# A hybrid SSD and attention block on one core: the softmax sums go from VectorE's adds to products of TensorE, the exponentials' products are spread among the projections, and the router's constants come from one product

## The chip, the cores and the metric

The kernel runs on 1 core of one Trainium2 chip. The metric is the device time in microseconds (us) of one execution; the median of 3 runs of the kernel before is 916.55 us (916.28 to 917.62). In the profile PE is TensorE, DVE is VectorE, ACT is ScalarE, POOL is GpSimd and SP is the engine whose queue issues most transfers.

## What is computed

One layer of a diffusion backbone over 512 latent tokens with a prefix of 256 context tokens, in float32: a modulated input projection, a bidirectional state-space scan (SSD), grouped-query attention, one output projection, a layer norm, and a mixture of experts (16 experts, two for each token), with a second layer norm. The change lies in attention and in the constants of the router:

```python
def gqa_block_attention(q, k, v):
    ...
    def one_block(q_blk):
        s = jnp.einsum('bqhgd,bkhd->bhgqk', q_blk, k, preferred_element_type=F32) * scale
        pr = jax.nn.softmax(s, axis=-1).astype(v.dtype)
        return jnp.einsum('bhgqk,bkhd->bqhgd', pr, v)
...
def hier_moe(h, p):
    ...
    g_prob = jax.nn.softmax((t @ p['w_rg'] + p['b_rg']).astype(F32), axis=-1)
    e_logits = (t @ p['w_re'] + p['b_re']).astype(F32).reshape(-1, MOE_GROUPS, EXPERTS_PER_GROUP)
    ...
```

There are 16 query heads on 4 key heads of 64 channels, and 768 keys (256 of the context, 512 latent).

## The kernel before, in words

The block runs in stages: the input projections and the scan (to about 411 us of the profiled span), attention with the output projection (411 to 690 us), the end of the router and the gathering of the tokens (690 to 712 us), then the experts. A list scheduler orders each engine's instructions by a priority (`tc.cur_priority`, which `rank` sets for a block of code) and by which operands and buffers it expects to be ready; each engine then works through its list in that order.

Attention (`attention`, L887) works in 16 units `u`, each one key head `kv` and one tile of 128 queries with the four query heads of that key head. The loop over `i` at L1050 steps through them, four steps to a unit, with several units under way at once. For a unit it does, in turn:

- `scores` (L931), four groups of one query head: a product of 512 and one of 256 keys into PSUM tile `s`, from which DVE takes the maximum of each query (`mx`, L943).
- `shift` (L945): DVE splits the maximum into two parts (`mhl`), TensorE turns them over by a product with the identity into a buffer `b`, and DVE writes the negated rows under the queries (L952).
- `weights` (L958): for each of six blocks of 128 keys two products of 512 columns into a buffer `b`, the first over 128 rows and the second over 72, with the maximum taken off by the last eight rows; ACT writes the exponential to `PT` (L967, tile `hxh`). `pb()` gives the buffers `b`, of which PSUM has two; `shift`, `weights`, the turned queries (`q_turn`, L921) and `finish` share them.
- `values` (L971): for each block two products of 256 columns, each with the 64 channels of `vv` as weights, which write the upper and the lower 64 partitions of tile `v` or `s`. Two blocks are asked for in each of three steps.
- `sums` (L980): DVE adds the six blocks of exponentials in three instructions (`ad`, L982 to L984). `norms` (L986) sums over the keys by 16 products of one column, 32 weight columns each, takes the reciprocal (`rc`) and spreads it (`rcb`).
- `finish` (L998): TensorE turns `rcb` into a buffer `b` (L1001), ACT copies it (`rb`, L1003), DVE multiplies (`o`, L1005), ACT and DVE split the result (`ah`, L1007, `al`, L1008).
- `project` (L1012): for each of two halves `n` of the output columns six products of 512 columns into tile `t`, and DVE adds them to the rows (L1026).

In the table of instructions a product of float32 operands, as `values` and `norms` have them, is two MATMUL entries; a product of float32r operands and a turn is one. All products are recorded at line 107, so groups are told apart by their tiles.

`out_group` for the second half of the scan's rows (`t<-whi,a`) and `router_prep` (L851) are given a place 150 priorities into attention. `router_prep` scales the router's weights by the modulation and the layer norm's gain (L868 to L874, tiles `wrA` and `xo`), and then sums them over the 1024 channels by 2 x 16 products with a tile of ones, 64 weight columns and 20 columns each. The router's constants `ca` and `cb` are read some 160 us later.

Of the kernel before, what the change touches and what calls it, by code (L numbers as in the profile page):

```python
# [8 lines left out]
F32 = mybir.dt.float32  # L9
# [84 lines left out]
def hybrid_block_kernel(ctx: ExitStack, tc: tile.TileContext, I, out):  # L94
# [756 lines left out]
    def router_prep():  # L851
        zero = xo[0][:, 0:256]
# [11 lines left out]
        SP.dma_start(w3[:, :, 4:20], I["w_re"].rearrange("(k p) n -> p k n", p=128))  # L864
        p = pb("t")
# [6 lines left out]
        V.tensor_add(cl[:, 24:32], cl[:, 24:32], cl[:, 8:16])  # L872
        V.tensor_tensor(wrA, w3, cl[:, 16:24, None].to_broadcast([128, 8, 20]), op=OP.mult)
        V.tensor_tensor(tmp, w3, cl[:, 24:32, None].to_broadcast([128, 8, 20]), op=OP.mult)  # L874
        p = pb("t")
        for j, w in enumerate((wrA, tmp)):
            for k in range(8):
                for a in range(2):
                    o = slice(a * 64, a * 64 + 64)
                    mm(p[o, j * 20:j * 20 + 20], ones[:, o], w[:, k], k == 0, k == 7)  # L880
# [4 lines left out]
    LAG, HOLD, WX = 150, 40, 3  # L885

    order = [(kv, t) for kv in (0, 1) for t in range(4)] + [(2, 0), (2, 1), (2, 2), (3, 0), (2, 3), (3, 1), (3, 2), (3, 3)]  # L887

    def attention():
# [6 lines left out]
        k2[0] = eap.tile([128, 2, 768], F32R, name="kT")  # L896
        kT = {}
# [47 lines left out]
        def shift(u):  # L945

            m = wo.tile([128, 8], F32R, name="mhl")
            V.tensor_copy(m[:, 0:4], mx[u])
            V.tensor_sub(m[:, 4:8], mx[u], f32(m[:, 0:4]))
            p = pb("b")[64:72, 0:128]  # L950
            mm(p, f32(m), ident, True, True)
            V.tensor_tensor(qB[u][64:72].rearrange("p (g q) -> p g q", g=4),  # L952
                            p[:, None, :].to_broadcast([8, 4, 128]),
                            minus[:, :, None].to_broadcast([8, 4, 128]), op=OP.mult)
# [3 lines left out]
        def weights(u, ks):  # L958

            kv = order[u][0]  # L960
            if 0 in ks:
                PT[u] = big[:, u % 2]
            for k in ks:
                p, o = pb(), slice(k * 128, (k + 1) * 128)
                mm(p, kT[kv][:, 0, o], qA[u], True, False)
                mm(p, kT[kv][0:72, 1, o], qB[u][0:72], False, True)
                S.activation(PT[u][:, k], p, AF.Exp)  # L967

        po, ad = {}, {}

        def values(u, ks):  # L971
            kv = order[u][0]
            if 0 in ks:
                po[u] = pb("s") if u % 2 else pss.tile([128, 512], F32, name="v")
            for k in ks:
# [36 lines left out]
        def project(u, n):  # L1012
# [19 lines left out]
            if kv == 3:  # L1032
                V.bn_stats(st6[:, t, n, :], us_[t][:, c])

        with rank(rowed):
# [13 lines left out]

        for i in range(4 * 16 + 26):  # L1050
# [3 lines left out]
            if u is not None:  # L1054
# [7 lines left out]
                if g == 3 and u + 1 < 16:  # L1062
                    q_turn(u + 1, qs.pop(u + 1))
            u, g = step(i, 4, 1)
            if u is not None:
                shift(u)
            u, g = step(i, 6, 4)
            if u is not None:
                weights(u, ((0,), (1, 2), (3, 4), (5,))[g])
            u, g = step(i, 10, 4)  # L1070
            if u is not None:
                if g == 0:
                    sums(u)
                if g < 3:
                    values(u, (2 * g, 2 * g + 1))
            u, g = step(i, 14, 1)
            if u is not None:
                rcb[u] = norms(u)
# [3 lines left out]
            u, g = step(i, 18, 2)  # L1082
            if u is not None:
                project(u, g)
# [11 lines left out]
    router_prep()  # L1096
# [578 lines left out]
```

## Time and profile before

| | |
|---|---|
| median of 3 runs | 916.55 us (916.28 to 917.62) |
| profiled execution | 912.09 us, span from first to last instruction 909.8 us |
| PE busy | 819.1 us (90%), 4974 products |
| DVE busy | 696.8 us (77%) |
| ACT busy | 420.2 us (46%) |
| POOL busy | 319.8 us (35%) |
| granted TensorE clock, mean | 0.964 of full speed |

A busy time is the time in which an engine has at least one instruction under way. Products overlap, so what one of them costs is read from its start to the start of the next. Times in the views below count from the first instruction. In a timeline the columns are start, duration, engine, line, operation, out<-in, shape and count, and in brackets the engine's idle time before it with the instruction that ended it. The letters `t`, `b`, `s`, `v` ahead of the arrow are the PSUM tiles named above.

### The profile page before, as it was taken

What the parts mean: (1) busy time and instruction counts of PE and PEld (TensorE: products, weight loads), DVE (VectorE), ACT (ScalarE), POOL (GpSimd) and SP (SyncE); (2) the same over time, 40 slices, a digit from 0 to 9 for tenths busy, and PEclk for the clock granted to TensorE, in tenths of its full rate; (3) what the DMA queues carried; (4) which work ended last, traced back from release to release, by engine and by line L of the source; (5) the groups of instructions that cost most, each with busy time, mean ns of one, the idle gap of its engine ahead of it and who ended that gap; (6) DMA issues with size and microseconds to landing.
All of it is one profiled execution on the core that took longest, in us unless ns stands there. A gap on an engine that the chain in (4) does not pass through costs nothing. (4 is left out here: it accounts for less than half of the span.)

```text
span 909.8 us, 13605 instructions
## 1 busy us (share of the span) xinstructions
PE 819.1 (90%) x4974; PEld 569.0 (63%) x4974; DVE 696.8 (77%) x1074; ACT 420.2 (46%) x776; POOL 319.8 (35%) x230
## 2 busy tenths in 40 slices
PE   6999998899989999999988999899982799999992
PEld 2696676556776566776655656556652577777762
DVE  3575764886967897656776787877888999899977
ACT  2253443545563144453541444444433466776652
POOL 0012211426231273410059036540314555545524
PEclk9999999999999999999997999999996799999997
DMA  9966996436343133676053011120185999999974
GB/s 300 319 195 235 286 303 215 128 116 185 104 118 83 45 118 109 202 227 170 24 151 103 13 30 62 46 83 1 53 273 207 332 350 340 331 339 343 338 212 192
DMA packets 112349, 165.54 MB, mean 182 GB/s; under 512 B 13144, under 2 KB 78200, under 8 KB 112280
## 3 DMA queue, kind: packets, MB, share of 16 engines
q1 hardware_dynamic: 105560, 141.24, 48.8%
q0 software_dynamic: 6288, 21.84, 8.4%
q10 hardware_dynamic: 432, 1.57, 0.5%
q8 instruction: 39, 0.64, 0.3%
q14 instruction: 30, 0.25, 0.1%
HBM read 142.41 MB, written 22.21 MB: 181 GB/s over the span
## 5 line engine op out<-in xcount | busy, mean ns | idle before, releaser
L75 ACT ACTIVATE whi<-wraw 128x1024 fp32r<-128x1024 f32 (+1 forms) x100 | 104.1, 1045 | 74.7 <-PE a L107 40.8
L76 DVE TENSOR_TENSOR wlo<-wraw,whi 128x1024 fp32r<-128x1024 f32 (+1 forms) x73 | 94.7, 1303 | 24.0 <-ACT whi L75 23.3
L967 ACT ACTIVATE hxh<-b 128x512 f32<-128x512 f32 x96 | 55.7, 595 | 88.9 <-PE b L107 88.2
L76 POOL TENSOR_TENSOR wlo<-wraw,whi 128x1024 fp32r<-128x1024 f32 (+1 forms) x22 | 53.5, 2432 | 117.9 <-ACT whi L75 98.5
L943 DVE TENSOR_REDUCE mx<-s 128x1 f32<-128x768 f32 x64 | 61.0, 953 | 34.3 <-PE s L107 34.2
L473 DVE SCALAR_TENSOR_TENSOR acc<-u,cols,acc 128x770 f32<-128x770 f32 (+1 forms) x48 | 56.8, 1182 | 28.5 <-ACT acc L465 23.0
L107 PE MATMUL a<-whi,hxh 128*128 128x512 f32 (+2 forms) x176 | 70.7, 403 | 1.8 <-ACT hxh L263 1.8
L107 PE MATMUL a<-wlo,hxh 128*128 128x512 f32 (+2 forms) x176 | 69.8, 397 | 0.2 <-DVE wlo L76 0.2
L107 PE MATMUL a<-whi,hxl 128*128 128x512 f32 (+2 forms) x176 | 69.1, 394 | 0.0
L107 PE MATMUL a<-hxl,whi 128*128 128x512 f32 (+1 forms) x176 | 64.5, 367 | 0.0
L107 PE MATMUL a<-hxh,whi 128*128 128x512 f32 (+1 forms) x176 | 64.1, 364 | 0.0
L107 PE MATMUL a<-hxh,wlo 128*128 128x512 f32 (+1 forms) x176 | 63.9, 363 | 0.0
L590 ACT ACTIVATE bc<-bc,lb 128x128 f32<-128x128 f32 x128 | 40.6, 392 | 13.5 <-POOL bc L587 13.3
L107 PE MATMUL a<-whi,xh 128*128 128x512 f32 x102 | 43.8, 429 | 0.0
L1435 POOL DMA_INDIRECT acc<-y,rowi x15 | 26.5, 1768 | 48.5 <-DVE wlo L76 29.6
L107 PE MATMUL a<-wlo,xh 128*128 128x512 f32 x102 | 41.1, 402 | 0.1
L107 PE MATMUL a<-whi,xl 128*128 128x512 f32 x102 | 40.9, 401 | 0.0
L107 PEld LDWEIGHTS a<-whi,hxh 128*128 128x128 f32 x176 | 33.9, 193 | 10.9 <-issue 4.2
L107 PEld LDWEIGHTS a<-wlo,hxh 128*128 128x128 f32 x176 | 34.0, 193 | 9.7 <-issue 4.9
L107 PEld LDWEIGHTS a<-hxh,wlo 128*128 128x128 f32 x176 | 33.9, 193 | 9.2 <-issue 5.3
L107 PEld LDWEIGHTS a<-whi,hxl 128*128 128x128 f32 x176 | 33.7, 192 | 9.3 <-issue 4.6
L107 PEld LDWEIGHTS a<-hxl,whi 128*128 128x128 f32 x176 | 34.0, 193 | 7.4 <-issue 3.6
(489 smaller groups left out, 2169.4 us busy)
## 6 DMA issues: line engine op xcount, KB each, us to landing
wraw<-in_w_mod_dram SPq DMA_DIRECT2D x32, 512.0 KB
wraw<-in_w_in_dram SPq DMA_DIRECT2D x30, 512.0 KB
wraw<-in_w_down_dram SPq DMA_DIRECT2D x22, 512.0 KB
wraw<-in_w_gate_dram SPq DMA_DIRECT2D x40, 256.0 KB
wraw<-in_w_up_dram SPq DMA_DIRECT2D x40, 256.0 KB
mraw<-in_w_mod_dram SPq DMA_DIRECT2D x32, 256.0 KB
bc<-csd SPq DMA_DIRECT2D x32, 256.0 KB
wraw<-in_w_out_dram SPq DMA_DIRECT2D x8, 512.0 KB
```

Of the source, the lines that this page charges most:

```text
L75: self.nc.scalar.activation(hi, raw, AF.Copy)
L76: self.lo_engine(i).tensor_sub(lo, raw, hi.bitcast(F32))
L107: return PE.matmul(o, lhsT=a, rhs=b, start=first, stop=last)
L473: V.scalar_tensor_tensor(a, uk, wk_, a, op0=OP.mult, op1=OP.add)
L590: S.activation(bc[:, d, h, :], bc[:, d, h, :], AF.Exp, bias=lb[:, c, h0 + h:h0 + h + 1])
L943: V.tensor_reduce(mx[u][:, g:g + 1], pss_[:, 768 * i:768 * i + 768], axis=AX, op=OP.max)
L967: S.activation(PT[u][:, k], p, AF.Exp)
L1435: G.indirect_dma_start(out=acc, out_offset=bass.IndirectOffsetOnAxis(ap=rows, axis=0), in_=y, in_offset=None, compute_op=OP.add)
```

## The change

It has three parts. (1) `sums` and the tile `ad` are gone. `values` now does all 12 products of a unit in one run, and behind them 48 products of one column (64 weight columns of `PT` against a column of ones), which sum the exponentials of all six blocks in PSUM; `norms` keeps only the reciprocal and `rcb`. The run has the rank of attention's start and is held until the last product of `weights` that was written before it. (2) `weights` does one block for each call, and a step sets one or two blocks between the four halves of `project`, which is now a generator; `shift` writes the split maximum into a part of the constants' tile and turns 72 columns over with one transpose; `finish` stands ahead of `weights`. (3) `router_prep` is a generator whose parts come at steps 18, 21, 24 and 27; DVE sums the scaled weights over the eight blocks of channels, and one product with ones, 40 columns wide, does the rest.

```diff
     def router_prep():
...
+        yield
         p = pb("t")
         PE.transpose(p[:, 0:32], rw[0:32, 0:128], ident[0:32, 0:32])
...
+        yield
         V.tensor_tensor(wrA, w3, cl[:, 16:24, None].to_broadcast([128, 8, 20]), op=OP.mult)
         V.tensor_tensor(tmp, w3, cl[:, 24:32, None].to_broadcast([128, 8, 20]), op=OP.mult)
+        wsum = wr[:, 352:392]
+        for j, w in enumerate((wrA, tmp)):
+            V.tensor_reduce(wsum[:, j * 20:j * 20 + 20], w.rearrange("p k n -> p n k"), axis=AX, op=OP.add)
+        yield
         p = pb("t")
-        for j, w in enumerate((wrA, tmp)):
-            for k in range(8):
-                for a in range(2):
-                    o = slice(a * 64, a * 64 + 64)
-                    mm(p[o, j * 20:j * 20 + 20], ones[:, o], w[:, k], k == 0, k == 7)
+        mm(p[:, 0:40], ones, wsum, True, True)
+        yield
...
+    PREP = (18, 21, 24, 27)
...
         def shift(u):
-            m = wo.tile([128, 8], F32R, name="mhl")
-            V.tensor_copy(m[:, 0:4], mx[u])
-            V.tensor_sub(m[:, 4:8], mx[u], f32(m[:, 0:4]))
-            p = pb("b")[64:72, 0:128]
-            mm(p, f32(m), ident, True, True)
+            V.tensor_copy(mhl[:, 64:68].bitcast(F32R), mx[u])
+            V.tensor_sub(mhl[:, 68:72].bitcast(F32R), mx[u], mhl[:, 64:68])
+            p = pb("b")[:, 0:128]
+            PE.transpose(p[0:72], mhl, ident)
+            p = p[64:72]
...
-        def values(u, ks):
+        def values(u):
             kv = order[u][0]
-            if 0 in ks:
-                po[u] = pb("s") if u % 2 else pss.tile([128, 512], F32, name="v")
-            for k in ks:
-                for gp in range(2):
-                    mm(po[u][gp * 64:gp * 64 + 64, 0:256], vv[:, k, kv * 64:(kv + 1) * 64],
-                       PT[u][:, k, gp * 256:gp * 256 + 256], k == 0, k == 5)
-        def sums(u):
-            a = ad[u] = wo.tile([128, 3, 512], F32, name="ad", bufs=1)
-            V.tensor_add(a, PT[u][:, 0:3], PT[u][:, 3:6])
-            V.tensor_add(a[:, 0], a[:, 0], a[:, 1])
-            V.tensor_add(a[:, 0], a[:, 0], a[:, 2])
+            p = po[u] = pb("s") if u % 2 else pss.tile([128, 512], F32, name="v")
+            with rank(first), tc.issue_after(held["weights"].ins):
+                for k in reversed(range(6)):
+                    for gp in range(2):
+                        mm(p[gp * 64:gp * 64 + 64, 0:256], vv[:, k, kv * 64:(kv + 1) * 64],
+                           PT[u][:, k, gp * 256:gp * 256 + 256], k == 5, k == 0)
+                for g in range(4):
+                    for k in range(6):
+                        for o in (0, 64):
+                            mm(p[o:o + 64, 256 + g:257 + g], PT[u][:, k, g * 128 + o:g * 128 + o + 64], ones[:, 0:1], k == 0, k == 5)
         def norms(u):
-            a = ad.pop(u)
-            for g in range(4):
-                for o in range(0, 128, 32):
-                    mm(po[u][o:o + 32, 256 + g:257 + g], a[:, 0, g * 128 + o:g * 128 + o + 32], ones[:, 0:1], True, True)
...
             for kk in range(2):
                 mm3(p, h[:, kk], l[:, kk], wh[:, kk], wl[:, kk], kk == 0, kk == 1)
+                if kk == 0:
+                    yield
...
+            u, g = step(i, 16, 1)
+            if u is not None:
+                finish(u, rcb.pop(u))
+                proj[u] = outs(u)
             u, g = step(i, 6, 4)
-            if u is not None:
-                weights(u, ((0,), (1, 2), (3, 4), (5,))[g])
...
+            ks = () if u is None else ((0, 1), (2,), (3, 4), (5,))[g]
+            v, h = step(i, 18, 3)
+            for j in range(2):
+                if j < len(ks):
+                    weights(u, ks[j])
+                if v is not None and (h, j) != (2, 1):
...
+                    next(proj[v], None)
+            u, g = step(i, 11, 1)
             if u is not None:
-                project(u, g)
+                values(u)
+            u, g = step(i, 13 if i < 72 else 12, 1)
+            if u is not None and u not in rcb:
+                rcb[u] = norms(u)
```

How the instructions stand shows at three places. A row is one instruction, or several in a row with their count, with its line, its operation, out<-in and shape, and the semaphores that it waits for (named after the engine or the DMA queue that raises them).

TensorE in the middle of attention, before, from the turn of one unit's maximum to the first products of `norms`; `s<-hxh,hxl` are `values`, `b<-hxl` are `weights`, `s<-kT,hxl` are `scores`, L1001 is the turn in `finish`:

```order
L107 MATMUL b<-cst,mhl 8x128 [waits DVE_49,Activation_49]
L107 MATMUL b<-hxl 128x512 [waits Activation_49]
L107 MATMUL b<-hxl 128x512
L107 MATMUL s<-hxh,hxl 64x256 x3
L107 MATMUL b<-hxl 128x512 [waits Activation_49]
L107 MATMUL b<-hxl 128x512
L107 MATMUL s<-hxh,hxl 64x256
L107 MATMUL s<-kT,hxl 128x256 [waits DVE_49]
L107 MATMUL s<-kT,hxl 128x512
L1001 MATMUL b<-cst,rcb 128x128 [waits DVE_49]
L1001 MATMUL b<-cst,rcb 128x128
L107 MATMUL s<-ones,ad 32x1 x5
```

The same engine now, at the run of one unit's values; `v<-ones,hxh` are the new sums, `t<-whi,ah` and the rows like it are `project`:

```order
L107 MATMUL b<-hxl 128x512 [waits Activation_49]
L107 MATMUL b<-hxl 128x512
L107 MATMUL v<-hxh,hxl 64x256 x12
L107 MATMUL v<-ones,hxh 64x1 x48
L107 MATMUL t<-whi,ah 128x512 [waits DVE_49]
```

The 12 products of values stand together, where they were parted into runs of 4, 3, 1 and 4, and the 48 one-column products follow them without another kind of product between.

TensorE now, from one unit's `shift` (L957) and the turn in `finish` (L1000) over the next products of `weights`:

```order
L957 MATMUL b<-cst 72x128 [waits DVE_49,PE_49,Activation_49]
L1000 MATMUL b<-cst,rcb 128x128 [waits Activation_49]
L1000 MATMUL b<-cst,rcb 128x128
L107 MATMUL b<-hxl 128x512 [waits Activation_49]
L107 MATMUL b<-hxl 128x512
L107 MATMUL s<-kT,hxl 128x256 [waits DVE_49]
L107 MATMUL s<-kT,hxl 128x512
L107 MATMUL b<-hxl 128x512 [waits Activation_49]
L107 MATMUL b<-hxl 128x512
L107 MATMUL b<-hxl 128x512 [waits DVE_49]
L107 MATMUL b<-hxl 128x512
```

The two turns now stand back to back, where before products of `weights` and `values` stood between them; of the next three pairs of `weights` two wait for ACT and the third for DVE.

DVE at the router's constants, before; L868 to L874 are `router_prep`, `mx<-s` are the maxima of `scores`, `mhl` and `qs` belong to `shift` and `q_stack`:

```order
L868 COPY xo<-t 128x32 [waits PE_49]
L943 TENSOR_REDUCE mx<-s 128x1
L869 TENSOR_SCALAR xo<-xo 128x8 [waits DVE_49]
L948 CAST mhl<-mx 128x4 [waits DVE_49]
L871 TENSOR_TENSOR xo<-xo 128x8 [waits DVE_49]
L871 TENSOR_TENSOR xo<-xo 128x8
L949 TENSOR_TENSOR mhl<-mx,mhl 128x4 [waits DVE_49]
L873 TENSOR_TENSOR wrA<-xo 128x160 [waits DMAHW3_49,DMAHW2_49,DVE_49]
L872 TENSOR_TENSOR xo<-xo 128x8 [waits DVE_49]
L874 TENSOR_TENSOR xo<-xo 128x160 [waits DVE_49]
L917 TENSOR_TENSOR qs<-q,qs 128x4x64 [waits DMAHW2_49,PE_49,Activation_49]
```

And now; L870 to L880 are `router_prep`, L1027 is the add of `project`:

```order
L870 COPY xo<-t 128x32 [waits PE_49]
L871 TENSOR_SCALAR xo<-xo 128x8 [waits DVE_49]
L950 TENSOR_REDUCE mx<-s 128x1 [waits PE_49]
L873 TENSOR_TENSOR xo<-xo 128x8 [waits DVE_49]
L873 TENSOR_TENSOR xo<-xo 128x8
L876 TENSOR_TENSOR wrA<-xo 128x160 [waits DMAHW3_49,DVE_49]
L874 TENSOR_TENSOR xo<-xo 128x8 [waits DVE_49]
L1027 TENSOR_TENSOR x<-x,t 128x512 [waits PE_49]
L877 TENSOR_TENSOR xo<-xo 128x160 [waits DVE_49]
L880 TENSOR_REDUCE xo<-wrA 128x20
L880 TENSOR_REDUCE xo<-xo 128x20 [waits DVE_49]
L950 TENSOR_REDUCE mx<-s 128x1 [waits PE_49]
```

The add of one half of `project` (L1027) now stands behind six of the router's instructions, and the next maximum behind three more.

## Rows read from the trace of the kernel before

**Rows 1.** Busy time by stretch: bounds, length; PE, PEld, DVE, ACT, POOL; clock, DMA.

```profile
410.00:490.00 80.00, 71.89 (x429) 46.99 (x429) 57.08 (x74) 29.60 (x50) 27.43 (x15) 0.94 0.40 114
490.00:650.00 160.00, 153.94 (x1145) 95.81 (x1144) 122.90 (x185) 68.53 (x139) 53.82 (x28) 0.99 0.13 39
650.00:690.00 40.00, 34.37 (x302) 22.63 (x301) 33.79 (x79) 16.62 (x29) 12.18 (x12) 0.91 0.69 237
```

**Rows 2.** Timeline of PE over one unit of attention.

```profile
554.34 0.50 PE L107 MATMUL t<-whi,ah 128*128 128x512 f32 x1
...
557.17 1.08 PE L107 MATMUL s<-hxh,hxl 128*64 128x256 f32 x8
558.18 0.50 PE L107 MATMUL t<-whi,ah 128*128 128x512 f32 x1
...
560.59 0.39 PE L107 MATMUL b<-cst,mhl 128*8 128x128 f32 x2
560.90 0.73 PE L107 MATMUL b<-hxl,kT 128*128 128x512 f32 x2
561.56 1.08 PE L107 MATMUL s<-hxh,hxl 128*64 128x256 f32 x6
562.57 0.73 PE L107 MATMUL b<-hxl,kT 128*128 128x512 f32 x2
563.23 0.65 PE L107 MATMUL s<-hxh,hxl 128*64 128x256 f32 x2
563.81 0.62 PE L107 MATMUL s<-kT,hxl 128*128 128x256 f32 x2
...
564.58 0.29 PE L107 MATMUL s<-ones,ad 128*32 128x1 f32 x10
564.79 1.20 PE L107 MATMUL b<-hxl,kT 128*128 128x512 f32 x4
...
566.27 1.08 PE L107 MATMUL v<-hxh,hxl 128*64 128x256 f32 x8
567.29 0.36 PE L107 MATMUL s<-ones,ad 128*32 128x1 f32 x22
567.58 0.50 PE L107 MATMUL t<-whi,ah 128*128 128x512 f32 x1
```

**Rows 3.** Timeline of PE at one tile's router logits (64 weight columns, 20 columns each).

```profile
680.44 1.11 PE L107 MATMUL t<-wrA,xo 128*64 128x20 f32 x32
681.48 0.50 PE L107 MATMUL s<-whi,ah 128*128 128x512 f32 x1
```

**Rows 4.** Timeline, a product of weights to its exponential, a turn to its copy.

```profile
574.11 0.74 PE L107 MATMUL b<-hxl,kT 128*128 128x512 f32 x2
...
574.89 0.60 ACT L967 ACTIVATE hxh<-b 128x512 f32<-128x512 f32 x1 [1.92 <-PE b L107]
...
577.48 0.38 PE L1001 MATMUL b<-cst,rcb 128*128 128x128 f32 x2
...
577.90 0.38 ACT L1003 ACTIVATE rb<-b 128x256 f32<-128x256 f32 x1 [0.75 <-PE b L1001]
```

**Rows 5.** Waits of PE from 410 to 690 us: total, times, longest.

```profile
PE t L107 <- DVE wrA L873: 3.5, 1, 3.5
PE b L107 <- DVE mhl L949: 3.3, 3, 1.4
PE t L107 <- DVE xo L874: 3.3, 1, 3.3
PE s L107 <- DVE o L1005: 1.9, 1, 1.9
PE t L107 <- DVE y L1026: 1.4, 1, 1.4
```

**Rows 6.** Timeline of DVE, two adds of the same shape.

```profile
525.80 0.69 DVE L983 TENSOR_TENSOR ad<-ad 128x512 f32<-128x512 f32 x1
...
527.01 2.67 DVE L984 TENSOR_TENSOR ad<-ad 128x512 f32<-128x512 f32 x1
```

More of the change, by code (lines that the diff above doesn't have):

```diff
@@ L896, in attention @@
         k2[0] = eap.tile([128, 2, 768], F32R, name="kT")
+        mhl = rows[:, 0:72]
+        V.memset(mhl[:, 0:64], 0.0)
         kT = {}
@@ L956, in attention, with weights @@
         PT = {}
-        def weights(u, ks):
+        def weights(u, k):
             kv = order[u][0]
-            if 0 in ks:
-                PT[u] = big[:, u % 2]
-            for k in ks:
[L964 to L969, printed above, removed]
-        def values(u, ks):
-            kv = order[u][0]
-            if 0 in ks:
-                po[u] = pb("s") if u % 2 else pss.tile([128, 512], F32, name="v")
-            for k in ks:
-                for gp in range(2):
-                    mm(po[u][gp * 64:gp * 64 + 64, 0:256], vv[:, k, kv * 64:(kv + 1) * 64],
-                       PT[u][:, k, gp * 256:gp * 256 + 256], k == 0, k == 5)
@@ L980, in sums @@
-        def sums(u):
-            a = ad[u] = wo.tile([128, 3, 512], F32, name="ad", bufs=1)
-            V.tensor_add(a, PT[u][:, 0:3], PT[u][:, 3:6])
-            V.tensor_add(a[:, 0], a[:, 0], a[:, 1])
-            V.tensor_add(a[:, 0], a[:, 0], a[:, 2])
+            PT[u] = big[:, u % 2]
+            p, o = pb(), slice(k * 128, (k + 1) * 128)
+            mm(p, kT[kv][:, 0, o], qA[u], True, False)
+            held["weights"] = mm(p, kT[kv][0:72, 1, o], qB[u][0:72], False, True)
+            S.activation(PT[u][:, k], p, AF.Exp)
@@ new lines, in attention @@
+        po = {}
+        def values(u):
+            kv = order[u][0]
+            p = po[u] = pb("s") if u % 2 else pss.tile([128, 512], F32, name="v")
[8 more added lines that the diff above has]
+                            mm(p[o:o + 64, 256 + g:257 + g], PT[u][:, k, g * 128 + o:g * 128 + o + 64], ones[:, 0:1], k == 0, k == 5)
@@ L1033, in project @@
                 V.bn_stats(st6[:, t, n, :], us_[t][:, c])
+            yield
+        first = tc.cur_priority
         with rank(rowed):
@@ L1048, in step, with outs @@
             return (u, g) if 0 <= u < 16 and g < n else (None, None)
+        proj = {}
+        def outs(u):
+            for n in range(2):
+                yield from project(u, n)
         for i in range(4 * 16 + 26):
@@ L1063, in attention @@
                     q_turn(u + 1, qs.pop(u + 1))
+            if i in PREP:
+                next(prep, None)
             u, g = step(i, 4, 1)
@@ L1066, in attention @@
                 shift(u)
-            u, g = step(i, 6, 4)
-            if u is not None:
-                weights(u, ((0,), (1, 2), (3, 4), (5,))[g])
[L1070 to L1078, printed above, removed]
             u, g = step(i, 16, 1)
@@ L1081, in attention @@
                 finish(u, rcb.pop(u))
-            u, g = step(i, 18, 2)
+                proj[u] = outs(u)
+            u, g = step(i, 6, 4)
+            ks = () if u is None else ((0, 1), (2,), (3, 4), (5,))[g]
[4 more added lines that the diff above has]
+                if v is not None and (h, j) != (2, 1):
+                    if (h, j) == (1, 0):
+                        pass
+                    next(proj[v], None)
+            u, g = step(i, 11, 1)
             if u is not None:
-                project(u, g)
+                values(u)
+            u, g = step(i, 13 if i < 72 else 12, 1)
+            if u is not None and u not in rcb:
+                rcb[u] = norms(u)
             u, g = step(i, 19, 4)
@@ L1095, in hybrid_block_kernel @@
             out_group(1, n)
-    router_prep()
+    prep = router_prep()
+    next(prep)
     tc.cur_priority = at
```

## The prediction

> **What bounds the kernel now.** I read the busy time by stretch first. From 490 to 650 us, the middle of attention, PE is busy 153.94 of 160 us and DVE 122.90 [rows 1], so PE's own work sets the pace, and DVE matters where PE waits for it. Next comes PE's timeline over one unit: from 554.34 to 567.58 us, 13.24 us, PE has no idle time in any row shown [rows 2]. Last come PE's waits: two of 3.5 and 3.3 us for the router's constants, and 3.3, 1.9 and 1.4 us in total for DVE's `mhl`, `o` and `y` [rows 5]. The granted clock is below 1 only near such waits: 0.94, 0.99 and 0.91 in the three stretches [rows 1]. Of its two levels (1.2 and 2.4 GHz) the lower is what PE gets after them.
>
> Two things follow. What the change adds to PE's list counts in full. What it takes from DVE counts only where a wait of PE goes with it. Attention's end releases the router's end and the experts, so a shift there passes to the span. Up to attention, and among the experts, the lists are the same.
>
> **The change part by part.** *The values' run.* The unit's 12 products (24 entries) take four runs now: 1.01, 1.01, 0.58 and 1.02 us from first start to the next group's [rows 2], 3.62 us. The run of six entries takes as long as that of eight, because its third product has no partner in the other column half. A step (one product, or two side by side) costs (1.01 - 0.58) / 2 = 0.215 us, and a run 0.15 us on top. One run of six pairs would have 12 steps (two entries each product): 12 x 0.215 + 0.15 = 2.73 us, which saves 0.89. Entering a run also delays the products ahead of it: a pair of `weights` takes 0.66 us at 560.90 and at 562.57, against 1.04 / 2 = 0.52 where two pairs follow each other at 564.79 [rows 2]. Three entries fewer save 3 x 0.14 = 0.42.
>
> *The sums.* The old ones cost PE 0.21 us (564.58) and 0.29 us (567.29) [rows 2], 0.50 in all. The new ones are 48 products, 96 entries, with 64 weight columns and one moving column. No row of before has that shape. The nearest have 64 weight columns and 20 moving: 32 entries from 680.44 to 681.48, 1.04 us [rows 3], between (1.04 - 0.15) / 32 = 27.8 and 32.5 ns each. The other bound is one moving column on 32 weight columns: 22 entries in 0.29 us, 13 ns each [rows 2]. I take 29 ns: with so few moving columns the weights must set the pace, they are the same width as in rows 3, and half that width costs about half. 96 x 29 ns = 2.78 us. Bounds: 96 x 13 ns = 1.25 and 96 x 32.5 ns = 3.12 us.
>
> A page of the Trainium skill would price them otherwise: TensorEngine Tiling (Array Packing), section Instruction Overhead, says that a matmul has some 60 cycles of overhead, so that one column takes as long as 60. By it, 96 entries at 25 ns (2.4 GHz) would be 2.4 us, an estimate from that page, and the sum below would be 6 us lower. Entries at 13 ns [rows 2] show that it does not hold across column groups that work side by side.
>
> *The shift.* The product with the identity, two entries of 128 columns, takes 0.31 us (560.59) [rows 2]; the one transpose that takes its place is one such entry, so about half: 0.16 saved.
>
> For one unit: -0.89 - 0.42 - 0.50 - 0.16 + 2.78 = +0.81 us; for 16, **+13.0 us**. Nothing hides it, PE being the bound. Before the first projections there are other broken runs, so I use the one price throughout.
>
> *A new wait.* Now the turn of the maximum and that in `finish` stand back to back and hold both buffers `b`; the next two pairs of `weights` wait for ACT, the third for DVE (order of the change). From the start of the turns to ACT's copy `rb` it takes 0.42 us, the copy 0.38 [rows 4], so the first pair can start 0.80 us after the turns, where PE is free after 0.31 (two turns of 128 columns, priced as the two entries at 560.59 [rows 2]): a wait of 0.49. From the pair's start to its exponential it takes 0.78 us, plus 0.60 [rows 4]: the same buffer is free 1.38 us later, at 2.18. PE has the pair itself (0.52) and a group of scores to do (0.46: from 563.81 to 564.58 it is 0.77 with two turns in it [rows 2], less their 0.31), to 1.78: a wait of 0.40. With a hand-over each, 1.0 us a unit. The list has the pattern in 10 units, once more in part: **+10.5 us**. Behind the waiting products stand `scores`, so DVE's maxima come later too; they are asked for only a unit later, and I cost that at nothing. Bounds: 0, if the buffers come free sooner than I think, and 16.
>
> *The router.* 64 entries of 29 ns go, 1.9 us; the one product left costs under 0.2. PE's waits of 3.5 and 3.3 us [rows 5] and the half clock behind them are at stake: 0.06 of 80 us is 4.8 us of clock [rows 1], of which some 1.6 fell on idle time, so 3.2: 10.0 us in all. They arose because DVE's small multiplications were held: an add of the same shape took 2.67 us where its neighbour took 0.69 [rows 6]. The Trainium skill's SBUF - State Buffer, section SBUF: two separate sides, gives the reason: a DVE operation with two SBUF inputs and a POOL operation that reads SBUF lock each other out. The four multiplications are still there, at the same place behind the second half of the scan's rows, and the add of the projection, which frees tile `t`, now stands behind six router instructions. PE's second projection waits for that add. At 2 us for each held multiplication that is again 6 to 7 us of waiting, in place of 6.8. I take -2 of the 10, so **-3.9 us** with the products; bounds -11.9 and -1.9.
>
> *DVE's adds.* Gone with them are PE's waits for `mhl`, `o` and `y`, 6.6 us [rows 5], which followed when those adds were held (the 2.67 us of [rows 6] ends just ahead of one). The clock gives 0.01 x 160 = 1.6 us, and half of 0.09 x 40 = 1.8, the other half belonging to the end of the router [rows 1]. That is 10.0 us. The splits `al` and `qs` stay and can be held as well; I leave 1.5: **-8.5 us**, bounds -10 and -3.
>
> **Sum:** 13.0 + 10.5 - 3.9 - 8.5 = +11.1 us. Against the profiled execution's 912.09 us that is 923.2. That execution is 4.46 us under the median of the runs, 916.55; moved by the same amount the median becomes **927.7 us**. A measurement tells about 0.2%, 1.8 us, from no change.
>
> **The rivals.**
> (a) *Cheap sums, faster.* If one moving column costs 13 ns on 64 weight columns too, the sums take 1.25 us a unit, 16 x 1.53 = 24.5 us less: 903.2. It decides from 2.78 - (11.1 + 1.8) / 16 = 1.97 us a unit, 20.5 ns an entry. For it: the old sums' entries start 13 ns apart. Against it: they have half the weight columns. 0.07.
> (b) *The buffers don't bind.* ACT and DVE release them in time, -10.5: 917.2, no change. For it: DVE has 3 us a unit less to do. Against it: the waits named are for ACT, whose chain of copy and exponential has no slack in it. 0.15.
> (c) *The router no longer stops PE.* -8: 919.7. For it: four steps lie between its parts. Against it: DVE's list, and POOL's work at that place is the same. 0.12.
> (d) Both (b) and (c): 909.2, faster. 0.10.
> (e) *More waits.* `al` or `qs` held by POOL while both buffers are taken, +8: 936. 0.08.
>
> **How the numbers follow.** The forecast has 0.48. Faster: (a), (d) and a third of (b), 0.22. Same: the rest of (b) and the near edge of the forecast's bounds, 0.09. Slower: 0.69. The range 908 to 936 takes in (b) to (d) and most of (e), and leaves out (a) and half of (e). The likeliest case's own range is 921 to 933.
>
> **What would show it.** In the profile after: the new sums' 96 entries take 2.7 to 2.9 us from first start to the next group's; the values' run takes 2.5 to 2.7; PE idles, or its products start late, by about 1 us behind the turns in `finish`; the unit is near 15 us instead of 13.24; PE waits over 4 us for DVE between the router's turn and its product; no DVE add takes over 2 us ahead of `mhl`. It is wrong if the unit is under 14 us, or if the sums start under 20 ns apart.

## The result and the profile after

The changed kernel takes 956.31 us (median of 4 runs, 955.73 to 963.41); the kernel before took 917.09 us beside it. The ratio is 1.043, with a 95% interval of 1.039 to 1.047: slower, as forecast, but by 39 us where 11 were forecast, and outside the range of 908 to 936.

| | before | after |
|---|---|---|
| profiled execution, span | 912.09, 909.8 us | 955.73, 953.9 us |
| PE busy, MATMUL entries | 819.1 us, 4974 | 854.5 us, 5920 |
| DVE busy | 696.8 us | 664.3 us |
| ACT, POOL busy | 420.2, 319.8 us | 420.8, 321.4 us |
| granted clock, mean | 0.964 | 0.931 |
| last product of attention's projections starts | 685.73 us | 724.98 us |

Of the 44 us that the two profiled spans lie apart (the profiled execution before is 5 us under its median), 39.2 lie before the last of attention's projections, and 4.9 behind it. The busy time by stretch, with the same bounds as [rows 1]:

```profile
410.00:490.00 80.00, 76.62 (x610) 58.56 (x610) 44.32 (x63) 31.85 (x57) 13.86 (x10) 0.94 0.37 103
490.00:650.00 160.00, 147.63 (x1432) 113.02 (x1432) 84.24 (x125) 54.03 (x109) 64.96 (x32) 0.84 0.16 49
650.00:690.00 40.00, 38.40 (x386) 29.53 (x388) 19.58 (x50) 16.13 (x31) 0.57 (x1) 0.91 0.03 9
```

DVE is busy 84.24 of 160 us in the middle of attention in place of 122.90: the relief that was meant is there. PE is busy less too, 147.63, though it has 287 entries more to do in that time. What is new is the clock, 0.84 where it was 0.99. One unit on PE, with the views of [rows 2]:

```profile
561.06 0.41 PE L957 MATMUL b<-cst 128*72 128x128 f32 x1
561.27 0.63 PE L1000 MATMUL b<-cst,rcb 128*128 128x128 f32 x2
562.38 0.73 PE L107 MATMUL b<-hxl 128*128 128x512 f32 x2 [0.47 <-ACT rb L1002]
...
563.79 1.21 PE L107 MATMUL b<-hxl 128*128 128x512 f32 x4 [0.34 <-ACT hxh L972]
...
566.59 0.50 PE L107 MATMUL t<-whi,al 128*128 128x512 f32 x1 [0.29 <-DVE al L1007]
...
569.34 2.81 PE L107 MATMUL s<-hxh,hxl 128*64 128x256 f32 x24
571.99 2.92 PE L107 MATMUL s<-ones,hxh 128*64 128x1 f32 x96
574.83 0.50 PE L107 MATMUL t<-whi,ah 128*128 128x512 f32 x1
575.16 0.39 PE L107 MATMUL t<-ml,ah 128*128 128x512 f32 x1
575.39 0.50 PE L107 MATMUL t<-whi,al 128*128 128x512 f32 x1
575.69 0.63 PE L107 MATMUL t<-whi,ah 128*128 128x512 f32 x1
576.11 0.63 PE L107 MATMUL t<-ml,ah 128*128 128x512 f32 x1
...
577.61 0.41 PE L957 MATMUL b<-cst 128*72 128x128 f32 x1
```

The unit, here from one turn of the maximum to the next, takes from 561.06 to 577.61, 16.55 us, where it took 13.24. The values run in one piece, 24 entries in 2.65 us, and the sums, 96 entries, in 2.84 us, 29.6 ns each. The pair of `weights` behind the turns waits 0.47 us for ACT's `rb`, the next 0.34 for the exponential, and a product of the projection 0.29 for `al`. And then there is what the prediction had not: the products at 575.16 and 575.39 are 0.23 and 0.30 us apart, those from 575.69 on 0.42, though no idle time stands ahead of any of them. The same stretch by windows (PE first, the granted clock behind POOL):

```profile
569.34:571.99 2.65, 2.65 (x26) 1.78 (x27) 1.96 (x4) 1.44 (x4) 2.01 (x1) 1.00 0.61 227
571.99:574.83 2.84, 2.84 (x98) 2.82 (x95) 0.00 (x0) 0.00 (x0) 1.37 (x2) 1.00 0.14 46
574.83:575.53 0.70, 0.70 (x7) 0.62 (x4) 0.18 (x1) 0.00 (x0) 0.00 (x0) 1.00 0.00 0
575.53:578.95 3.42, 2.95 (x11) 2.01 (x9) 1.71 (x3) 0.46 (x2) 0.97 (x1) 0.50 0.00 0
```

PE is busy without a break through the values and the sums, at full clock; 0.7 us behind the sums the clock falls to half (1.2 of 2.4 GHz) for 3.4 us. It is the same at 14 of the 16 pieces of sums: by the clock records of the trace a stretch of half clock begins no later than 1.5 us behind their end, at three of them while the piece still runs. The Trainium skill, TensorE: Matmul & The Clock Gate, section Why this matters for your kernels, asks that TensorE be kept busy without idle gaps between bursts, so that its clock doesn't fall. By the busy column of these rows that was done, and the clock fell; what PE did just before was 96 entries of one column each.

PE's waits from 410 to 690 us, as in [rows 5], and DVE's timeline at the router, first `xo` multiplications, then the projection's add:

```profile
PE b L107 <- ACT rb L1002: 4.7, 10, 0.5
PE t L107 <- DVE x L1027: 3.8, 1, 3.8
PE b L107 <- ACT hxh L972: 2.9, 9, 0.3
...
PE t L107 <- DVE xo L870: 1.0, 1, 1.0
```

```profile
489.69 1.61 DVE L873 TENSOR_TENSOR xo<-xo 128x8 f32<-128x8 f32 x2
...
491.50 2.30 DVE L874 TENSOR_TENSOR xo<-xo 128x8 f32<-128x8 f32 x1
493.73 0.67 DVE L1027 TENSOR_TENSOR x<-x,t 128x512 f32<-128x512 f32 x1
```

The waits for `mhl`, `o` and `y` are gone from this window (attention now goes on to 725 us, and there PE waits 0.9 + 1.5 us for `y`). Those for the turns have come, 4.7 + 2.9 us. At the router a wait of 3.8 for the add at 493.73, which stands behind multiplications of 128x8 that take 1.61 us (two) and 2.30 (one), has taken the place of the two of 3.5 and 3.3.

**Where the time went.** The table is worked out from all of PE's products between 411 us and the last of attention's projections: each counts from its start to the next start, less the idle time ahead of that; where the granted clock was half, half of it is put under "clock". (That is somewhat too much where a hand-over takes as long at full clock; the rest of the run with 32 columns, 4.4 us over the change's, gives an idea of it.) Idle is the time in which no product is under way. Each column is one execution, and those of one kernel differ: the kernel before took 912.6 to 925.0 us, and the run with the router alone, which changes no sums, shows 14.3 us under "clock" where the kernel before shows 7.9. So differences of a few us between columns are not read as effects.

| us, from 411 | before | after | 32 columns | sums in two | adds back | idle entries in before |
|---|---|---|---|---|---|---|
| in all | 274.5 | 313.8 | 298.4 | 292.9 | 257.3 | 349.6 |
| sums | 7.6 | 45.3 | 45.9 | 46.7 | 7.0 | 53.0 |
| values | 59.0 | 42.3 | 42.2 | 42.2 | 44.0 | 62.3 |
| clock | 7.9 | 36.5 | 8.2 | 15.4 | 13.0 | 36.2 |
| idle | 18.9 | 21.7 | 29.8 | 20.1 | 23.6 | 17.1 |
| the rest | 181.0 | 167.9 | 172.3 | 168.5 | 169.6 | 180.9 |

From before to after: sums +37.7, values -16.7, clock +28.6, idle +2.8, the rest -13.1 us: +39.3. Without the clock the sum would be +10.7, but that is arithmetic and no time: in the run with 32 columns, whose clock is as before, attention is 23.9 us longer than before, as PE then waits more.

### The profile page after: what moved, and what is told of

Read it like the earlier page. It is cut to its first block, busy times and chain, and to the rows that moved or that the text cites. A ratio compares the mean times of both kernels' runs of the same rounds, so it can differ in the third digit from the quotient of the medians.

```text
span 953.9 us, 15450 instructions
## 1 busy us (share of the span) xinstructions
PE 854.5 (90%) x5920; PEld 629.2 (66%) x5920; DVE 664.3 (70%) x1029; ACT 420.8 (44%) x776; POOL 321.4 (34%) x230
## 3 DMA queue, kind: packets, MB, share of 16 engines
q1 hardware_dynamic: 105560, 141.24, 46.7%
HBM read 142.41 MB, written 22.21 MB: 173 GB/s over the span
## 5 line engine op out<-in xcount | busy, mean ns | idle before, releaser
L76 DVE TENSOR_TENSOR wlo<-wraw,whi 128x1024 fp32r<-128x1024 f32 (+1 forms) x73 | 98.7, 1357 | 22.1 <-ACT whi L75 20.8
L1002 ACT ACTIVATE rb<-b 128x256 f32<-128x256 f32 x16 | 6.1, 384 | 105.8 <-PE b L1000 105.8
L1450 POOL DMA_INDIRECT acc<-y,rowi x15 | 29.7, 1979 | 53.8 <-DVE xl L1405 23.1
L921 POOL TENSOR_TENSOR q<-q,rsq 128x256 f32<-128x256 f32 x16 | 10.8, 676 | 97.7 <-DMA q<-q_d 80.5
L107 PE MATMUL b<-hxl,kT 128*128 128x512 f32 x96 | 38.2, 489 | 2.8 <-ACT rb L1002 1.9
```

The costliest lines, as they stand in the source:

```text
L76: self.lo_engine(i).tensor_sub(lo, raw, hi.bitcast(F32))
L107: return PE.matmul(o, lhsT=a, rhs=b, start=first, stop=last)
L921: G.tensor_tensor(heads(q, 4), heads(q, 4), r, op=OP.mult)
L1002: S.activation(rb, p, AF.Copy)
L1450: G.indirect_dma_start(out=acc, out_offset=bass.IndirectOffsetOnAxis(ap=rows, axis=0), in_=y, in_offset=None, compute_op=OP.add)
```

## The experiments

The theory: the sums cost what they were priced at, and besides this the clock falls because of them: 48 products of one column, though PE shows as busy throughout. Rivals: the clock falls because of the unbroken run of the values, or because of the waits behind the turns. "Before" in each ratio is the kernel before, run on the same chip beside it; its median lay between 916.5 and 919.9 us, so small differences between two experiments are better read from the ratios.

**The adds back.** In the changed kernel, the sums as they were:

```diff
-                for g in range(4):
-                    for k in range(6):
-                        for o in (0, 64):
-                            mm(p[o:o + 64, 256 + g:257 + g], PT[u][:, k, ...], ones[:, 0:1], k == 0, k == 5)
+        def sums(u):
+            a = ad[u] = wo.tile([128, 3, 512], F32, name="ad", bufs=1)
+            V.tensor_add(a, PT[u][:, 0:3], PT[u][:, 3:6])
...
-            u, g = step(i, 13 if i < 72 else 12, 1)
+            u, g = step(i, 14, 1)
```

> The sums go back to DVE's three adds and 16 products of one column; the unbroken run of the values, the order of the exponentials and the stepped router stay. Theory (the 96 entries of one column cost their 2.8 us a unit, and leave PE so little busy that the clock falls to half behind them): about 16 x (2.84 - 0.5) = 37 us of PE's list go, and some 22 us of half clock; DVE's held adds give back up to 8: 900 to 908 us, and no half clock of 3.41 us in step with the units. Rival (the half clock comes from the unbroken run of the values, or from the waits behind the two turns): the same 37 us go, the half clock stays in step with the units: 918 to 928 us.

899.86 us, ratio to before 0.977 (0.973 to 0.981): 56 us under the change, and faster than both kernels. The clock's share falls from 36.5 to 13.0 us, with the unbroken values still there and the two turns still back to back, so neither is its cause. In the middle of attention the clock is 0.95, where the change has 0.84:

```profile
490.00:650.00 160.00, 146.10 (x1153) 100.69 (x1153) 143.62 (x214) 70.86 (x140) 66.79 (x35) 0.95 0.20 63
```

The adds stand one step of the loop later than in the kernel before. Attention ends 17.3 us sooner than before; some 9 us of it are lost behind: at the first gathering PE waits 12.3 us, where it was 4.2 before.

```profile
PE b L1410 <- DMA x<-t_d,toki: 12.3, 1, 12.3
```

**The sums thinned.** 8 products in place of 48; the division by the sums is left out:

```diff
-                for g in range(4):
-                    for k in range(6):
-                        for o in (0, 64):
-                            mm(p[o:o + 64, 256 + g:257 + g], PT[u][:, k, ...], ones[:, 0:1], k == 0, k == 5)
+                for g in range(4):
+                    for o in (0, 64):
+                        mm(p[o:o + 64, 256 + g:257 + g], ones[:, o:o + 64], ones[:, 0:1], True, True)
```

> The 96 entries of the sums are 16 (weights are ones in place of the exponentials, so the softmax is not divided by its sums: that part of the computation is left out). All else as in the change. Theory: 80 x 29.5 ns x 16 = 38 us go, and with them some 22 us of half clock: 893 to 900 us. Rival (values' run or waits cause the half clock): 38 us go, the half clock stays: 916 to 920 us.

936.34 us in all, outside both ranges, but this total can't be used: the attention's result is another one, so other rows go to the experts (146.08 MB are read from HBM, where the change reads 142.41), and from the last projection on the run takes 261 us, where the change takes 229. Up to that product it takes 262.6 us, 51.2 less than the change: 37.1 of the sums, 26.0 of the clock, while idle rises by 8.8 and the rest by 3.4. Behind none of the 16 pieces does the clock fall. That is the theory's case, with part of it given back.

**32 columns in place of one.** The same products in the same order, each with more to move:

```diff
-                            mm(p[o:o + 64, 256 + g:257 + g], PT[u][:, k, ...], ones[:, 0:1], k == 0, k == 5)
+                            mm(p[o:o + 64, 256 + 32 * g:256 + 32 * g + 32], PT[u][:, k, ...], ones[:, 0:32], k == 0, k == 5)
...
-            V.reciprocal(rc, po[u][:, 256:260])
+            V.reciprocal(rc, po[u][:, 256:256 + 128].rearrange("p (g n) -> p g n", g=4)[:, :, 0])
```

> Each product of the sums moves 32 columns of ones in place of one; count, order and result are the same. Theory: the entries still take about 29 to 33 ns (the weights set the pace), and the half clock behind them is gone because the columns keep PE busy: 2.8 to 3.2 us a unit, 932 to 942 us. Rival 1 (the half clock does not depend on the columns of the sums): 956 to 962 us with the same half clock. Rival 2 (one column was cheap by its columns, and 32 cost in proportion): the run takes well over 4 us a unit, over 965 us.

939.19 us, ratio 1.021 (1.016 to 1.025). PE's timeline, and the middle of attention by windows:

```profile
561.85 0.50 PE L107 MATMUL t<-whi,al 128*128 128x512 f32 x1 [0.89 <-DVE al L1007]
...
567.25 2.94 PE L107 MATMUL s<-ones,hxh 128*64 128x32 f32 x96
570.12 0.50 PE L107 MATMUL t<-whi,ah 128*128 128x512 f32 x1
570.46 0.40 PE L107 MATMUL t<-ml,ah 128*128 128x512 f32 x1
570.69 0.39 PE L107 MATMUL t<-whi,al 128*128 128x512 f32 x1
...
572.07 0.38 PE L1000 MATMUL b<-cst,rcb 128*128 128x128 f32 x2
```

```profile
490.00:650.00 160.00, 143.80 (x1544) 109.34 (x1544) 84.90 (x129) 58.99 (x117) 61.09 (x30) 0.95 0.14 43
```

96 entries of 32 columns take 2.87 us, as long as those of one, and the projections behind them follow each other in 0.23 us: the clock is 0.95 in place of 0.84. This is the plainest of the runs: each of the 96 entries moves 31 columns more, in the same time, and the kernel takes 17 us less. Behind none of the 16 pieces does the clock fall. Nothing but the columns differs (and which columns the reciprocal reads), so the half clock came with the one column. Of the 28.3 us of clock 15.3 come back as time: idle is 8.1 higher (the wait for `al` is now 0.89 us where it was 0.29) and the rest 4.4.

**The turns apart.** `finish` is asked for behind `weights`, at the end of the step, as before the change:

```diff
-            u, g = step(i, 16, 1)
-            if u is not None:
-                finish(u, rcb.pop(u))
-                proj[u] = outs(u)
...
+            u, g = step(i, 16, 1)
+            if u is not None:
+                finish(u, rcb.pop(u))
+                proj[u] = outs(u)
             u, g = step(i, 19, 4)
```

> The turns of finish are asked for at the end of the step, so they no longer stand right behind the turn of the maximum; the sums stay. Theory: the waits of 0.47, 0.34 and 0.29 us behind the turns, in 10 units, go: 8 to 11 us, 945 to 949 us, and the half clock behind the sums stays. Rival 1 (those waits lower the clock): half clock goes too, 920 to 928 us. Rival 2 (the wait only moves, since ACT's chain of copy and exponential is what PE follows): 954 to 958 us.

951.60 us, ratio 1.033 (1.029 to 1.037); the change's was 1.043. That is 4.7 us under the change by the medians and some 9 by the ratios, so the total doesn't tell the theory from the second rival. PE's waits do, from 410 to 690 us:

```profile
PE b L107 <- ACT hxh L972: 8.2, 11, 1.8
PE t L107 <- DVE x L1027: 6.1, 2, 5.8
...
PE b L107 <- ACT rb L1002: 0.6, 1, 0.6
```

The wait for `rb` is gone but for 0.6 us, and those for the exponentials have risen from 2.9 to 8.2: idle is 22.0 us in all, not less than 21.7. So the second rival is right about the waits, they only move. What is gained stands under clock (28.0 after 36.5), not under the 8 to 11 us of waits. The half clock stays behind 11 of the 16 pieces of sums, against the first rival.

**Both, adds back and turns apart** (the two edits above together).

> Both at once: the sums back on DVE (as in the run with the adds back) and the turns of finish asked for at the end of the step. Theory (the waits behind the two turns are PE's own loss, whatever the sums are): 5 to 8 us less than the 899.9 us with the adds back alone: 892 to 895 us. Rival (PE follows ACT there, or the experts' start is held by the gathers): 898 to 902 us.

902.23 us, ratio 0.984 (0.981 to 0.987): no gain over the adds back alone (0.977), as the rival said. What the prediction took for the turns doesn't come back when they are apart.

**The router alone**, in the kernel before: `router_prep` of the change, with its steps, and nothing else.

> The kernel before with the router's constants alone in steps and by one product. Theory (as predicted: the waits for the router stay, the 64 entries go): 3 to 5 us under before, 0.3 to 0.6%. Rival 1 (the steps take PE's waits of 3.5 and 3.3 us and the half clock behind them away): 8 to 11 us under before. Rival 2 (a wait as long behind another product): no change, within 0.2%.

916.35 us, ratio 0.998 (0.995 to 1.001). That excludes a gain of 8 to 11 us; between the theory's 3 to 5 and nothing it doesn't tell. The wait for DVE at the router stays, 4.7 us in one piece.

**The values alone**, in the kernel before:

```diff
-                if g < 3:
-                    values(u, (2 * g, 2 * g + 1))
+            u, g = step(i, 11, 1)
+            if u is not None:
+                values(u)
```

> The kernel before with the values' products alone in one run (15 of 16 units), sums on DVE as before. Theory (a run saves 1.0 to 1.3 us a unit, and an unbroken run does not lower the clock): 16 to 21 us under before, no half clock in step with the units. Rival 1 (the unbroken run lowers the clock): half clock of 3.41 us in most units, less than 8 us under before. Rival 2 (PE then waits for ACT and DVE instead): 6 to 12 us under before, with the waits of PE up by as much as the run saves less.

913.19 us, ratio 0.997 (0.995 to 1.000). The products of the values do fall from 59.0 to 43.9 us, and the clock stays (10.4 us after 7.9); idle rises from 18.9 to 27.5 and the rest from 181.0 to 184.3. The second rival, and more of it than it said:

```profile
PE b L107 <- ACT hxh L967: 6.9, 11, 0.7
PE t L107 <- DVE wrA L873: 5.9, 1, 5.9
```

PE waits 6.9 us for exponentials, where it waited 0.4 before; the 5.9 for the router, in one piece, were 3.5 + 3.3 before.

**No spread of the exponentials**, with the adds back and the turns apart:

```diff
+                for k in ((0,), (1, 2), (3, 4), (5,))[g]:
+                    weights(u, k)
...
+                for j in range(2):
+                    next(proj[u], None)
```

> The kernel with the adds back and the turns apart (902.2 us), its exponentials' products again in groups of one and two and its projections whole, as before the change. Theory (the unbroken run of the values saves 15 us of PE's list, but it is given back as waits for ACT's exponentials unless single products of weights stand between halves of projections): about the time of the values' run alone, 908 to 916 us, with PE's waits up by 5 to 10 us over the run with the spread. Rival (the spread does nothing, and what the run with the values alone lacked was the turn of the maximum or the router): 898 to 904 us.

904.38 us, ratio 0.985 (0.979 to 0.990), where the same with the spread took 902.23. That is the rival's case, within the noise: the order of the exponentials is worth nothing that this can tell. What the run with the values alone lacked, 9 us, must lie in what still parts the two kernels: the router, the turn of the maximum, and the places of the adds and of `finish` in the loop. Which of them was not tried.

**Entries that do nothing, in the kernel before.** 48 products behind the sums' own, in one piece:

```diff
-                    mm(po[u][o:o + 32, 256 + g:257 + g], a[:, 0, ...], ones[:, 0:1], True, True)
+                    last = mm(po[u][o:o + 32, 256 + g:257 + g], a[:, 0, ...], ones[:, 0:1], True, True)
+            with rank(first), tc.issue_after(last.ins):
+              for g in range(4):
+                for k in range(6):
+                    for o in (0, 64):
+                        mm(po[u][o:o + 64, 260 + 1 * g:260 + 1 * g + 1], a[:, 0, g * 128 + o:g * 128 + o + 64], ones[:, 0:1], k == 0, k == 5)
```

> The kernel before with 48 further products (96 entries of one column on 64 weight columns) in one piece behind the sums' own, in each unit; their results are not used, the values' runs stay broken, the turns apart. Theory (such a piece costs 2.84 us by itself, and lowers the clock whatever the values' run and the turns do): 45 us of PE's list and some 15 us net of half clock, 55 to 65 us over before, half clock of 3.41 us in most of the 16 units. Rival (the half clock needs the unbroken run of the values ahead of the sums, or the turns back to back): 42 to 48 us over before, half clock in few units.

999.11 us, ratio 1.093 (1.089 to 1.097), 82 over before. Here the values' runs are broken and the turns apart, and the clock falls all the same (the 118 entries are 22 of the old sums and the 96):

```profile
560.96 1.08 PE L107 MATMUL s<-hxh,hxl 128*64 128x256 f32 x6
...
566.70 3.26 PE L107 MATMUL s<-ones,ad 128*32 128x1 f32 x118
...
570.70 0.39 PE L107 MATMUL t<-whi,ah 128*128 128x512 f32 x1
570.93 0.52 PE L107 MATMUL t<-ml,ah 128*128 128x512 f32 x1
571.24 0.63 PE L107 MATMUL t<-whi,al 128*128 128x512 f32 x1
571.67 0.84 PE L107 MATMUL s<-kT,hxl 128*128 128x256 f32 x2
```

The last products at 570.70 and 570.93 are 0.23 us apart; from 571.24 on they take 0.43. The clock falls during or right behind 12 of the 16 pieces, and its share is 36.2 us, as in the change. So one-column products alone suffice. The time is over what was expected, since hardly any of the half clock is hidden by shorter waits: idle falls by only 1.8 us.

**The sums in two pieces.** 24 products behind the values, 24 behind the scores after the turns:

```diff
-                for g in range(4):
+                for g in range(2):
...
         def norms(u):
...
+            last = held["half"].ins
+            with rank(first), tc.issue_after(last):
+                for g in range(2, 4):
+                    for k in range(6):
+                        for o in (0, 64):
+                            mm(p[o:o + 64, 256 + g:257 + g], PT[u][:, k, ...], ones[:, 0:1], k == 0, k == 5)
```

> The change with its 48 products of the sums in two pieces of 24: one behind the values, one some 4 us later, behind the scores that follow the turns (13 of 16 units). Same products, same count. Theory (a whole piece leaves PE so little busy for 2.8 us that the clock falls; half a piece with full products around it does not): the half clock behind the sums goes for the most part, and the second piece lies where PE waited for ACT: 930 to 944 us. Rival (the number of such entries matters and not their being in one piece): the half clock stays, a switch more in each unit: 954 to 962 us.

936.35 us, ratio 1.018 (1.012 to 1.024), 20 us under the change with the same products:

```profile
560.17 1.52 PE L107 MATMUL s<-ones,hxh 128*64 128x1 f32 x48
561.61 0.50 PE L107 MATMUL t<-whi,ah 128*128 128x512 f32 x1
561.95 0.39 PE L107 MATMUL t<-ml,ah 128*128 128x512 f32 x1
...
563.57 0.38 PE L1007 MATMUL b<-cst,rcb 128*128 128x128 f32 x2
564.42 0.74 PE L107 MATMUL b<-hxl,kT 128*128 128x512 f32 x2 [0.47 <-ACT rb L1009]
565.00 0.54 PE L107 MATMUL s<-kT,hxl 128*128 128x256 f32 x2
565.47 1.57 PE L107 MATMUL s<-ones,hxh 128*64 128x1 f32 x48
566.97 1.22 PE L107 MATMUL b<-hxl,kT 128*128 128x512 f32 x4
```

```profile
490.00:650.00 160.00, 151.53 (x1593) 117.20 (x1594) 91.10 (x135) 59.23 (x118) 59.28 (x30) 0.93 0.13 41
```

The piece at 565.47 stands where PE waited 0.34 us for the exponential, and the pairs behind it no longer wait. In the middle of attention the clock is 0.93 after 0.84. The clock's share falls from 36.5 to 15.4 us, though the count of entries is the same and a switch more is paid in each unit (sums 46.7 after 45.3). In the three last units the sums are still in one piece, and behind two of these the clock falls. The theory's case.

**The router later**, with the adds back:

```diff
-    PREP = (18, 21, 24, 27)
+    PREP = (34, 38, 42, 46)
```

> The kernel with the adds back, and the router's steps asked for 16 steps of the loop later (34, 38, 42, 46 in place of 18, 21, 24, 27), where POOL has gaps of 7 to 9 us in place of work without a pause. Theory (the small multiplications are held only while POOL works beside them, and PE's products behind them wait for that): the multiplications of 128x8 take under 0.3 us each in place of 1.2 to 1.7, PE's waits there (some 4 us) and a half clock of 3.4 us go: 893 to 897 us. Rival (by the router's place nothing is lost that PE has not to wait for elsewhere): 898 to 902 us.

907.42 us, ratio 0.987 (0.982 to 0.992), 7.6 us slower than with the router early (0.977), which neither theory nor rival expected. DVE's multiplications are short now; the first two rows are of the run with the adds back, the others of this one:

```profile
476.05 2.40 DVE L873 TENSOR_TENSOR xo<-xo 128x8 f32<-128x8 f32 x2
...
478.97 1.74 DVE L874 TENSOR_TENSOR xo<-xo 128x8 f32<-128x8 f32 x1
```

```profile
526.72 0.23 DVE L873 TENSOR_TENSOR xo<-xo 128x8 f32<-128x8 f32 x2
...
527.55 0.16 DVE L874 TENSOR_TENSOR xo<-xo 128x8 f32<-128x8 f32 x1
```

Two take 0.23 us, one 0.16, in place of 2.40 and 1.74. They stand in POOL's gap of 7.7 us. That agrees with the reason that the prediction took from the Trainium skill, SBUF - State Buffer, section SBUF: two separate sides, where a DVE operation with two SBUF inputs and a POOL operation that reads SBUF lock each other out. And yet attention ends no sooner: its last projection starts 1.8 us later, and idle is 24.7 us where it was 23.6. So nothing is gained, as the rival said; the rest of the 7.6 us lies behind attention or in the noise, and was not followed.

## Why the prediction was wrong

The sign was right, and so were the two largest terms, the sums and the values. The step that failed is the reading of the clock, which gave the clock's term the wrong sign; the gain booked for DVE's adds didn't come either.

- *Sums*, 2.78 us a unit: measured 2.84 (+37.7 us for 16, forecast +36.5). An entry of one column takes 29.6 ns with 64 weight columns, and 29.9 with 32 columns to move, so the moving columns don't set the pace; that the weights do, as taken, fits PEld's 2.82 busy of the 2.84 us. By the Trainium skill, TensorEngine Tiling (Array Packing), section Instruction Overhead, the estimate was 2.4 us a unit; the trace says 2.84.
- *Values' run*, 2.73: measured 2.65. Values -16.7 us; `weights`, scores and projections, among them the products ahead of the runs, about -8.9, the turn of the maximum -3.5: 29.1 us, forecast 21.0 + 2.6.
- *The new wait*, 1.0 us a unit in ten units: it stands in the trace with 0.47 + 0.34 + 0.29. But the run with the turns apart shows no cost by itself: without it PE waits as long elsewhere (idle 22.0 after 21.7).
- *DVE's adds*, -8.5: the waits for `mhl`, `o` and `y` went as forecast up to 690 us, and no add of the projections takes over 0.7 us, but PE's idle time as a whole rose by 2.8 us nevertheless, and by 10.9 in the run with 32 columns, whose clock is as before. With the adds back it is 23.6. So the 6.6 us of named waits were no gain to be had: others stood behind them.
- *The router*, -3.9: the waits came out as forecast (4.8 us for DVE between its turn and its product). Alone it gives -0.2% (-0.5 to +0.1).
- *The clock.* Here lies the error. The prediction read that the clock is below 1 "only near such waits", took half clock to be what PE gets after waiting, and booked 3.4 us of gain for the waits to go, and part of 3.2 at the router. For the kernel before the reading is right: its four stretches of half clock between 411 and 690 us all begin beside a wait of 1.4 us or more. But that kernel has no run of over 32 one-column entries in attention, so its trace could not show what such a run does. Measured: +28.6 us of clock. PE busy without a gap for 2.84 us, with 96 entries of one column each, is followed by half clock. Shown from four sides: more columns in the same products (clock 8.2), the same products in two pieces (15.4), no such products (13.0), and such products in a kernel that has nothing else of the change (36.2). None of the rivals in the prediction had this; it would have taken one more question on the added 2.8 us: what does PE move in this time?
- *The sum.* That the table without its clock comes to +10.7, beside a forecast of +11.1, is luck: the products ahead saved more than forecast, and the waits counted on DVE's adds and the turns came out otherwise. Of the signs that it named, the unit of near 15 us failed: 16.55, with one stretch of 3.4 us of half clock in each, 1.7 us lost. A slip that decides nothing: "same" has 0.09, less than the 0.10 of the two thirds of (b) that fall there.

Besides, the experts' part is 4.9 us longer than before. It is 9 us longer with the adds back, where attention ended 17 us sooner, and there the wait for the first gathering is 8 us longer. In the changed kernel that wait is 1.0 us longer (5.2 after 4.2), and the mean clock of this part is 0.90 after 0.92; what makes it so was not tried.

## What to carry to other kernels

Price a run of narrow products twice: once by its entries, and once by what the clock does behind it. Where many such products can't be avoided, try giving each more columns where these cost nothing (here 32 for one: 17 us), or breaking the run up with full products (20 us), with the pieces put where PE waits anyway. Moving a sum from an engine that is not the bound to the one that is must win more than waits with a name; here the same change with the adds left on DVE is faster than the kernel before by 1.9 to 2.7%.

## What the runs showed that was not expected

- Clock and wait stand in for each other. With 28.3 us of clock given back (32 columns), attention was 15.3 us shorter; 8.1 us came back as PE's idle time, most of it waits for ACT and DVE that the slow clock had covered, as that for `al` (0.89 after 0.29).
- Two parts of the change that alone give 0.2 and 0.3% (router, values) give 1.5% together with the turn of the maximum (and the small moves in the loop named above); a part tried alone in a kernel with many waits behind one another says little.
- The experts' part took 224 to 236 us with the same rows and 261 with others, and not in step with when attention ends, so changes in attention are better compared at its own end.
